# A layer's constants loaded by a generator of their own, one transfer a step, and the gated norm's sums of squares 1.5 later, in a two-layer hybrid decoder trunk

## The chip, the cores and the metric

The kernel runs on one core of one Trainium2 chip. The metric is the device time of one execution in microseconds, taken as the median of the runs; lower is better. Times inside an execution are counted from the start of its span, which runs from its first instruction to its last.

Engines are named as the profile names them: PE (TensorE matmuls; PEld its weight loads), DVE (VectorE), ACT (ScalarE), POOL (GpSimd), SP (SyncE, which here only issues transfers). A name with a q behind it (ACTq, SPq) is the sequencer of that engine: the instructions that it handles itself, the issuing of transfers (DMAs) above all.

## What is computed

Two pre-norm residual layers over 256 tokens of width 1024, all in float32. Each layer normalises the stream, multiplies it with one wide input matrix, runs three causal token mixers beside each other, gates and projects each of them, merges them and adds the result to the stream.

```python
for layer in range(DEPTH):                                   # DEPTH = 2
    h = rms_norm(x, norm_w[layer])
    proj = jnp.einsum('bsd,de->bse', h, w_in[layer])         # 1024 -> 12832 columns
    (a_xbc, a_z, a_dt, b_q, b_k, b_v, b_z,
     c_q, c_k, c_v, c_f, c_z, gates) = jnp.split(proj, split_at, axis=-1)
    y_a = mamba2_branch(a_xbc, a_z, a_dt, conv_w[layer], conv_b[layer], dt_bias[layer],
                        a_log[layer], d_skip[layer], ssm_norm_w[layer])
    y_b = sliding_window_branch(b_q, b_k, b_v, b_z, sinks[layer], cos, sin)
    y_c = forgetting_attention_branch(c_q, c_k, c_v, c_f, c_z, f_bias[layer])
    branch = jnp.einsum('bsiw,iwd->bsid', jnp.stack([y_a, y_b, y_c], axis=2), w_proj[layer])
    g = jax.nn.sigmoid(gates.reshape(b, s, N_BRANCH, d) + gate_bias[layer])
    x = x + jnp.einsum('bsd,de->bse', jnp.sum(g * branch, axis=2), w_out[layer])
return rms_norm(x, final_norm_w)
```

The end of the first mixer is the gated norm that the change touches: four groups of 256 channels, each scaled by the inverse root of its mean square.

```python
y = y + d_skip * xh                                          # d_skip: one number a head
y = y * jax.nn.silu(z)
yf = y.reshape(b, s, 4, 256)
return (yf * lax.rsqrt(jnp.mean(yf * yf, axis=-1, keepdims=True) + NORM_EPS)).reshape(b, s, d) * norm_w
```

## The kernel before

**Tiling.** Weights come in pieces of 512 KB (`raw`, 128 partitions x 1024 numbers), six buffers deep, issued by SP (`load_to`, L336). Each piece is split into a rounded high part `hi` (ACT, L268) and a remainder `lo` (DVE, L269), six buffers each and at most four pieces ahead of PE (`AHEAD`, L32), and three matmul passes (hi x hi, lo x hi, hi x lo; `dense`, L282) give a float32 product. A raw buffer is free for the next transfer once its `lo` is made; a `hi` or `lo` buffer is free once PE has used it for the last time. The program is a list of operations (`ops`): each one computes 128 channels or 128 tokens of one piece into a PSUM buffer (`mm`, three of them), which ACT or DVE then reads. Small products, transposes and scores go to five other PSUM buffers (`mx`).

**Order of the work.** While it is written out, the program keeps a modelled PE time (`clock["t"]`, in microseconds, advanced by `mm` and `transpose`). Everything besides the dense products is a generator, here called a mixer: `launch(br, gen, delay)` (L103) enters it with the time from which it may run, and after each operation `pump` (L130) steps the mixers that are due, the one due longest first. A mixer yields a delay (the constants `D_...`) or a condition. `drain(br)` (L140) runs all mixers of the number `br` to their end at once. PE runs in the order in which this writes its instructions. The other engines are ordered by the scheduler, except for instructions given to `pin` (L262), which keep the order of the program among themselves; the transfers of the constants are pinned, on ACT's sequencer.

**Transfers.** SP issues the weights; ACT's sequencer issues the constants, the gate biases, the residual, and `cumd` and `bias` (the decays of two mixers, written out and read back in another shape). The build gives each of these transfers one of eight completion semaphores in turn, SP's and ACT's together, and a transfer waits on its own sequencer until the last one with the same semaphore has landed. An engine's sequencer goes on in order: while it waits to issue a transfer, the instructions behind it on that engine wait too.

**The constants of a layer** (`layer_consts`, L412 to L430): `vr` (convolution taps and biases, norm weights: 88 rows of 128), `hb` (four vectors of 16 numbers to all 128 partitions), `dsk` (d_skip, twice 64 partitions x 8 numbers; every second number of a row is taken, so each of the 512 numbers of a half is an element of its own in DRAM), and in layer 1 `nwb` (the norm weights, 512 KB, then multiplied by -0.5 on POOL). Layer 0 calls it behind the first key and value products (L1143), layer 1's constants are loaded in the middle of layer 0's third mixer (L1174). `layer_vec` (L432) transposes `vr` on PE and makes small vectors of `hb`; it stands ahead of the second mixer's gates in each layer. `dsk` is first used at L815, `nwb` at L1074.

**The gated norm** (`u_z` with `br == 0`, L838 to L857, and `group_norm`, L850 on): each pair of gates `z` adds the squares of its 256 channels (DVE L842), then launches `group_norm` with the delay `D_GN1`; that sums over the channels with four small products against `ones` on PE, and DVE L855, POOL L858 and DVE L860 to L863 make the scale `gr` of them, which the projection reads at L974 and L976. The line numbers of the kernel after the change are 11 higher from `layer_vec` on.

Of the kernel before, what the change touches and what calls it, by code (L numbers as in the profile page):

```python
# [14 lines left out]
ALU = mybir.AluOpType  # L15

P = 128
S = 256
D = 1024
NK = D // P  # L20
# [3 lines left out]

D_SOFT, D_SOFT2, D_EVAC, D_SSD, D_SSD2 = 7.0, 3.0, 3.0, 8.0, 3.0
D_K, D_Q, D_QK, D_G0, D_FOX, D_BDMA, D_BIAS = 6.0, 5.5, 2.0, 8.0, 0.0, 4.0, 2.0
D_SEL = 2.5
D_GN1, D_CUM, D_H, D_M = 5.0, 12.0, (4.8, 7.0), 5.0
BUDGET = 1.35
T_PP, T_SSD, T_BIAS = 1, 1, 1  # L30
N_RAW, N_SPLIT = 6, 6
# [13 lines left out]
def hybrid_trunk(  # L45
# [5 lines left out]
    nc = tc.nc  # L51
# [11 lines left out]
    def T(tag, shape, dtype=F32, bufs=None):  # L63
        count[0] += 1
        return sb.tile(shape, dtype, tag=tag, name=f"{tag}_{count[0]}",
                       bufs=bufs if bufs is not None else BUFS.get(tag, 1))

    def PS(tag, bufs):
        count[0] += 1
        return ps.tile([P, 512], F32, tag=tag, name=f"{tag}_{count[0]}", bufs=bufs)  # L70
# [4 lines left out]
    def pmx():  # L75
        return PS("mx", 5)
# [22 lines left out]
    def transpose(o, a, i):  # L99
        clock["t"] += 0.109  # L100
        nc.tensor.transpose(o, a, i)  # L101

    def launch(br, gen, delay=0.0):  # L103
        clock["n"] += 1
        waiting.append([clock["t"] + delay, clock["n"], br, gen, None])
# [12 lines left out]
    def allowed(m):  # L118
        return m[4] is None or (tokens[m[4]] > 0 if isinstance(m[4], str) else m[4]())
# [4 lines left out]
    def enter(m):  # L124
        if isinstance(m[4], str):
            tokens[m[4]] -= 1
        m[4] = None
        step(m)
# [11 lines left out]
    def drain(br):  # L140

        left = 0
        while any(m[2] == br for m in waiting):
            for m in sorted(waiting, key=lambda m: (m[0], m[1])):
                if m[2] == br and allowed(m):
                    left += 1
                    enter(m)
                    break
            else:
                m = min((m for m in waiting if allowed(m)), key=lambda m: (m[0], m[1]))  # L150
                left += 1
                enter(m)
        if left and VERBOSE:
            print("drained", br, left, "at", round(clock["t"], 1))
# [107 lines left out]
    def pin(f):  # L262
        return lambda *a, **k: tc.keep_in_program_order(f(*a, **k))  # L263
# [139 lines left out]
    for l in range(L):  # L403
        y = Layer()
# [5 lines left out]
    pdma = pin(nc.scalar.dma_start)  # L410

    def layer_consts(y):  # L412
        l = y.l
        vr = T("vr", [88, P])
        pdma(vr[0:64, :], conv_w[l].rearrange("j (u p) -> (j u) p", p=P))
        pdma(vr[64:80, :], conv_b[l:l + 1, :].rearrange("o (u p) -> (o u) p", p=P))
        pdma(vr[80:88, :], ssm_norm_w[l:l + 1, :].rearrange("o (u p) -> (o u) p", p=P))
        if l:
            y.nwb = T("nwb", [P, D])
            pdma(y.nwb, norm_w[l:l + 1, :].to_broadcast([P, D]))  # L420
            pin(nc.gpsimd.tensor_scalar)(y.nwb, y.nwb, -0.5, None, op0=ALU.mult)
        y.hb = T("hb", [P, 64], bufs=2)
        for i, v in enumerate((dt_bias, f_bias, sinks, a_log)):
            pdma(y.hb[:, 16 * i:16 * i + 16], v[l:l + 1, :].to_broadcast([P, 16]))
        y.dsk = T("dsk", [P, NK], bufs=2)
        for half in range(2):
            src = d_skip[l:l + 1, :].rearrange("o (j two) -> two o j", two=2)[half]
            pdma(y.dsk[64 * half:64 * half + 64, :], src.to_broadcast([64, NK]))
        y.vr = vr

    def layer_vec(y):
        p = pmx()  # L432
        transpose(p[:, 0:88], y.vr, ident[:88, :88])
        y.vec = T("vec", [P, 88], bufs=2)
        act(y.vec[:, 0:80], p[:, 0:80], AF.Copy, scale=0.5)
        act(y.vec[:, 80:88], p[:, 80:88], AF.Copy, scale=-0.5)
        y.nsink = T("nsink", [P, 16], bufs=2)
        pin(ts)(y.nsink, y.hb[:, 32:48], -1.0, None, op0=ALU.mult)
        y.nega = T("nega", [P, 16], bufs=2)
        pin(act)(y.nega, y.hb[:, 48:64], AF.Exp)  # L440
        pin(ts)(y.nega, y.nega, -1.0, None, op0=ALU.mult)
# [167 lines left out]
    def swa_quad(y, c, qT):  # L609
# [64 lines left out]
        tokens["pp"] += 1  # L674
        yield D_SEL
        yield lambda: (1, 2 * c + 1) in y.zdone
# [419 lines left out]
    def sub(src, n=256):  # L1096
        subs.append((src, n))
        return len(subs) - 1
# [5 lines left out]
    for y in layers:  # L1104
        l = y.l
# [32 lines left out]
        if l == 0:  # L1138
            k, v = cols(C_BK), cols(C_BV)
            op(k, u_bkv(y, 0, 0, [lambda j=j: second_rows(j) for j in range(2)]))  # L1140
            op(k, u_bkv(y, 0, 1))
            op(v, u_bkv(y, 256, 0), u_bkv(y, 256, 1))
            op(None, lambda: layer_consts(y0))  # L1143
            for c in (0, 2):
                op(cols(C_BQ + 256 * c, 512), u_bq(y, c, 0), u_bq(y, c, 1))
        else:
            kv, q0 = cols(C_BK, 512), cols(C_BQ)
            op(None, lambda: drain(5))
            op(kv, u_bkv(y, 0, 0))
            op(q0, u_bq(y, 0, 0))  # L1150
            op(None, lambda: drain(6))
            op(kv, u_bkv(y, 0, 1))
            op(q0, u_bq(y, 0, 1))
            for c, n in ((1, 512), (3, 256)):
                op(cols(C_BQ + 256 * c, n), u_bq(y, c, 0), u_bq(y, c, 1))
        op(None, lambda y=y: layer_vec(y))
        op(sub([(0, w[:, C_DT:C_DT + 16]), (16, w[:, C_CF:C_CF + 16])], 32), u_small(y))
        zs(C_ZB, 1)
# [11 lines left out]
        for b, zb in enumerate(((), (0,), (1,), (2, 3))):  # L1170
            op(cols(C_CK + 256 * b), u_ck(y, 2 * b, 0), u_ck(y, 2 * b + 1, P))
            op(cols(C_CQ + 256 * b), u_cq(y, 2 * b, 0), u_cq(y, 2 * b + 1, P))
            if b == 1:
                op(None, load_final if l + 1 == L else lambda: layer_consts(layers[1]))  # L1174
            for z in zb:
                z1(C_ZC, 2, z)
# [4 lines left out]
        o = [sub([(0, w_out[l, :, c:c + n])], n) for c, n in ((0, 256), (256, 512), (768, 256))]  # L1181
# [96 lines left out]
```

## Time and profile before

| what | us |
|---|---|
| median of 3 runs (840.38 to 842.8) | 840.53 |
| the profiled execution, its own device time | 841.65 |
| its span, first to last instruction | 839.8 |
| PE busy in it | 822.7 (98%) |
| DVE busy | 655.9 (78%) |
| ACT busy | 503.3 (60%) |
| POOL busy | 123.4 (15%) |
| DMA, mean | 189 GB/s |

The profile is one execution. Matmuls are pipelined and their ends are modelled, so that a busy PE may still be slowed, by its clock or by short waits between matmuls; a stage is best judged by the time between two points of the program that occur in both layers. "Idle before" in a row is the time that the engine stood before the first instruction of the row, with what ended it.

### The profile page before, as it was taken

Reading aid. Unit: us, or ns where it says so; the run is one execution under the profiler, and the core shown is the slowest. Engines: PE = TensorE matmul, PEld = TensorE weight load, DVE = VectorE, ACT = ScalarE, POOL = GpSimd, SP = SyncE. Lnnn points to the kernel's source line nnn. Section 1 sums busy time; section 2 is a strip of 40 time slices with the busy share of each in tenths; the row PEclk is TensorE's granted clock in tenths of the full one; section 3 lists DMA queues with packets and bytes.
Section 4 is the critical chain, followed back from the end, with each engine's and each line's share of the span. In section 5 each row is a group of like instructions: output and inputs, shape, how many; then the busy total and the mean of one; then the engine's idle time right before and its main releaser. Section 6 shows DMA issues by size and latency. Waiting matters only on the chain.

```text
span 839.8 us, 15652 instructions
## 1 busy us (share of the span) xinstructions
PE 822.7 (98%) x5800; PEld 749.8 (89%) x5800; DVE 655.9 (78%) x1355; ACT 503.3 (60%) x970; POOL 123.4 (15%) x167
## 2 busy tenths in 40 slices
PE   7999999999999999999999999999999999999996
PEld 6989888989989998888989998898899999888896
DVE  5778997998776678876688879979968668788665
ACT  6466777665556675544455668775556667655442
POOL 7411400000211101110014122000003110211000
PEclk9999999999999999999999999999999999999999
DMA  9576565567456546776577455556756564576632
GB/s 304 163 228 201 177 201 164 173 216 226 140 156 212 177 149 189 232 218 215 191 225 242 143 184 171 161 188 211 229 173 181 172 178 150 177 221 216 213 102 74
DMA packets 123595, 158.39 MB, mean 189 GB/s; under 512 B 12784, under 2 KB 84192, under 8 KB 123520
## 3 DMA queue, kind: packets, MB, share of 16 engines
q1 hardware_dynamic: 109456, 140.79, 53.9%
q10 hardware_dynamic: 14016, 16.49, 6.4%
q8 instruction: 45, 0.74, 0.4%
q14 instruction: 30, 0.25, 0.1%
q0 software_dynamic: 48, 0.13, 0.0%
HBM read 155.22 MB, written 2.16 MB: 187 GB/s over the span
## 4 chain that ended last, share of the span: by engine, by line
PE 82%; DVE 7%; DMA 4%; ACT 3%; issue 2%; POOL 1%; ACTq 1%; SPq 0%; POOLq 0%; DVEq 0%
PE mm L97 70%; PE mx L97 9%; DMA raw<-in_w_in_dram 4%; PE mx L101 3%; DVE lo L269 3%; ACT hi L268 1%; POOL sm L858 1%; DVE L L836 1%; DVE L L837 1%; DVE pp L577 1%; DVE pp L559 0%; ACT L L845 0%; ACTq L263 0%; ACT pp L565 0%; DVE L L842 0%
## 5 line engine op out<-in xcount | busy, mean ns | idle before, releaser
L269 DVE TENSOR_TENSOR lo<-raw,hi 128x1024 fp32r<-128x1024 f32 x252 | 310.8, 1247 | 77.4 <-ACT hi L268 71.9
L97 PE MATMUL mm<-hi,L 128*128 128x512 f32 (+1 forms) x1280 | 354.0, 363 | 1.8 <-ACT hi L1209 1.2
L97 PE MATMUL mm<-L,hi 128*128 128x256 f32 x1792 | 318.4, 279 | 0.9 <-DVE L L477 0.9
L268 ACT ACTIVATE hi<-raw 128x1024 fp32r<-128x1024 f32 x252 | 263.3, 1055 | 90.0 <-PE mm L97 68.3
L97 PEld LDWEIGHTS mm<-L,hi 128*128 128x128 f32 x1792 | 278.8, 193 | 6.9 <-issue 3.2
L97 PEld LDWEIGHTS mm<-hi,L 128*128 128x128 f32 x1280 | 229.2, 190 | 30.6 <-issue 2.4
L97 PE MATMUL mm<-L,lo 128*128 128x256 f32 x896 | 247.4, 276 | 0.0
L97 PE MATMUL mm<-lo,L 128*128 128x512 f32 (+1 forms) x640 | 229.4, 359 | 1.4 <-POOL lo L1210 1.4
L97 PEld LDWEIGHTS mm<-L,lo 128*128 128x128 f32 x896 | 172.7, 193 | 0.2
L97 PEld LDWEIGHTS mm<-lo,L 128*128 128x128 f32 x640 | 120.9, 189 | 15.4 <-POOL lo L1210 1.8
L908 POOL TENSOR_SCALAR_AFFINE_SELECT bias<-bias 128x128 f32<-128x128 f32 x64 | 37.3, 614 | 265.4 <-DMA bias<-cumd 265.3
L768 DVE SCALAR_TENSOR_TENSOR L<-L,vec,L 128x255 f32<-128x255 f32 (+2 forms) x96 | 46.9, 489 | 6.1 <-ACT L L765 4.8
L97 PE MATMUL mx<-L,L 128*64 128x128 f32 (+1 forms) x384 | 36.5, 332 | 0.0
L640 ACT ACTIVATE pp<-pp,nm 128x128 f32<-128x128 f32 x64 | 25.2, 394 | 15.6 <-DVE nm L633 12.6
L97 PEld LDWEIGHTS mx<-L,L 128*64 128x64 f32 x384 | 23.8, 137 | 11.9 <-issue 2.7
L565 ACT ACTIVATE pp<-pp,nm 128x128 f32<-128x128 f32 x64 | 28.2, 442 | 7.2 <-DVE nm L559 7.2
L932 ACT ACTIVATE L<-L 128x512 f32<-128x512 f32 x24 | 15.1, 627 | 29.0 <-DVE L L931 28.7
L829 ACT ACTIVATE L<-mm 128x256 f32<-128x256 f32 x48 | 18.0, 375 | 21.1 <-PE mm L97 17.4
L771 ACT ACTIVATE L<-L 128x256 f32<-128x256 f32 x32 | 13.4, 418 | 27.3 <-DVE L L768 26.9
L665 POOL TENSOR_SCALAR_AFFINE_SELECT L<-L 128x256 f32<-128x256 f32 x16 | 10.9, 680 | 107.7 <-ACT L L663 107.7
L633 DVE CUSTOM_DVE_ANT_0 pp<-mx,wmask,nsink 128x128 f32<-128x128 f32 x64 | 24.2, 413 | 1.8 <-PE mx L97 1.8
L858 POOL TENSOR_TENSOR sm<-sm,mhalf 128x4 f32<-128x4 f32 x8 | 10.9, 1363 | 91.8 <-DVE sm L855 91.8
(181 smaller groups left out, 820.8 us busy)
## 6 DMA issues: line engine op xcount, KB each, us to landing
raw<-in_w_in_dram SPq DMA_DIRECT2D x200, 512.0 KB, 4.7
raw<-in_w_proj_dram SPq DMA_DIRECT2D x48, 512.0 KB, 4.6
raw<-in_w_out_dram SPq DMA_DIRECT2D x16, 512.0 KB, 4.8
L<-cumd ACTq DMA_DIRECT2D x8, 512.0 KB, 4.4
bias<-cumd ACTq DMA_DIRECT2D x16, 256.0 KB, 3.7
L<-in_gate_bias_dram ACTq DMA_DIRECT2D x12, 256.0 KB, 3.6
L<-in_x_dram SPq DMA_DIRECT2D x2, 512.0 KB, 6.1
nwb<-in_norm_w_dram SPq DMA_DIRECT2D x1, 512.0 KB, 5.2
```

What stands on the lines that cost most here:

```text
L97: nc.tensor.matmul(o, a, b, **kw)
L101: nc.tensor.transpose(o, a, i)
L268: keep(act)(hi, src, AF.Copy)
L269: keep(tt)(lo, src, hi.bitcast(F32), op=ALU.subtract)
L565: act(pp[:, i, sl], pp[:, i, sl], AF.Exp, scale=-1.0, bias=nm[:, e:e + 1], accum_out=sums[:, e:e + 1])
L633: nc.vector.tensor_tensor_reduce(out=pp[:, i, sl], in0=score(p, i, b), in1=m, scale=-0.125, scalar=ns[:, i:i + 1], op0=ALU.add, op1=ALU.mi ...
L640: act(pp[:, i, sl], pp[:, i, sl], AF.Exp, scale=-1.0, bias=nm[:, e:e + 1], accum_out=sums[:, e:e + 1])
L768: stt(a[:, s:S], x_[:, 0:S - s], y.vec[:, 16 * j + u:16 * j + u + 1], a[:, s:S], op0=ALU.mult, op1=ALU.add)
L829: act(halves(th), p, AF.Tanh, scale=0.5)
L858: nc.gpsimd.tensor_tensor(r0[:, 0:4], v[:, 0:4], mhalf[:, 0:4], op=ALU.pow)
L908: nc.gpsimd.affine_select(out=bias[:, i, dst], in_=bias[:, i, src], compare_op=ALU.is_ge, fill=NEG, base=0, pattern=[[-1, P]], channel_mul ...
L932: act(g, g, AF.Tanh, scale=0.5)
```

## The change

`layer_consts` no longer issues its transfers in one go. It launches a mixer (number 9) that issues one transfer a step with 1.5 of modelled PE time between them (`D_CONST`), in another order: `hb` first, then `vr`, then `dsk`, and in layer 1 `nwb` last, in two halves with 10.0 behind each (`D_NWB`). `layer_vec` runs what is left of it before it uses the constants. `D_GN1` goes from 5.0 to 6.5.

```diff
-D_SEL = 2.5
-D_GN1, D_CUM, D_H, D_M = 5.0, 12.0, (4.8, 7.0), 5.0
+D_SEL, D_CONST, D_NWB = 2.5, 1.5, 10.0
+D_GN1, D_CUM, D_H, D_M = 6.5, 12.0, (4.8, 7.0), 5.0
...
     def layer_consts(y):
+        launch(9, consts(y))
+
+    def consts(y):
         l = y.l
-        vr = T("vr", [88, P])
-        pdma(vr[0:64, :], conv_w[l].rearrange("j (u p) -> (j u) p", p=P))
-        pdma(vr[64:80, :], conv_b[l:l + 1, :].rearrange("o (u p) -> (o u) p", p=P))
-        pdma(vr[80:88, :], ssm_norm_w[l:l + 1, :].rearrange("o (u p) -> (o u) p", p=P))
-        if l:
-            y.nwb = T("nwb", [P, D])
-            pdma(y.nwb, norm_w[l:l + 1, :].to_broadcast([P, D]))
-            pin(nc.gpsimd.tensor_scalar)(y.nwb, y.nwb, -0.5, None, op0=ALU.mult)
+        y.vr = T("vr", [88, P])
         y.hb = T("hb", [P, 64], bufs=2)
+        y.dsk = T("dsk", [P, NK], bufs=2)
         for i, v in enumerate((dt_bias, f_bias, sinks, a_log)):
             pdma(y.hb[:, 16 * i:16 * i + 16], v[l:l + 1, :].to_broadcast([P, 16]))
-        y.dsk = T("dsk", [P, NK], bufs=2)
+            yield D_CONST
+        pdma(y.vr[0:64, :], conv_w[l].rearrange("j (u p) -> (j u) p", p=P))
+        yield D_CONST
+        pdma(y.vr[64:80, :], conv_b[l:l + 1, :].rearrange("o (u p) -> (o u) p", p=P))
+        yield D_CONST
+        pdma(y.vr[80:88, :], ssm_norm_w[l:l + 1, :].rearrange("o (u p) -> (o u) p", p=P))
+        yield D_CONST
         for half in range(2):
             src = d_skip[l:l + 1, :].rearrange("o (j two) -> two o j", two=2)[half]
             pdma(y.dsk[64 * half:64 * half + 64, :], src.to_broadcast([64, NK]))
-        y.vr = vr
+            yield D_CONST
+        if l:
+            y.nwb = T("nwb", [P, D])
+            for j in range(2):
+                hs = slice(j * 512, (j + 1) * 512)
+                pdma(y.nwb[:, hs], norm_w[l:l + 1, hs].to_broadcast([P, 512]))
+                yield D_NWB
+            pin(nc.gpsimd.tensor_scalar)(y.nwb, y.nwb, -0.5, None, op0=ALU.mult)
 
     def layer_vec(y):
+        drain(9)
         p = pmx()
         transpose(p[:, 0:88], y.vr, ident[:88, :88])
```

Below, rows of the built program are shown at three places: an engine's instructions in its order, each with the tile that it writes and those that it reads; [waits DMAHW1_49] is a wait on one of the eight semaphores of transfers, other waits name the engine.

**ACT in layer 0, from the key transpose on** (`L_51` is the key tile, written once for each half of the tokens; `vr`, `hb`, `dsk` the constants; `hi` the split of weights). Before:

```order
L504 ACTIVATE L_51_267<-mx_397 128x4x128 [waits PE_49]
L263 DMA vr_403<-in_conv_w_dram 64x128
L263 DMA vr_403<-in_conv_b_dram 16x128
L263 DMA vr_403<-in_ssm_norm_w_dram 8x128
L263 DMA hb_407<-in_dt_bias_dram 128x16 [waits DMAHW7_49]
L263 DMA hb_407<-in_f_bias_dram 128x16 [waits DMAHW0_49]
L263 DMA hb_407<-in_sinks_dram 128x16 [waits DMAHW1_49]
L263 DMA hb_407<-in_a_log_dram 128x16 [waits DMAHW3_49]
L263 DMA dsk_412<-in_d_skip_dram 64x8x1 [waits DMAHW4_49]
L263 DMA dsk_412<-in_d_skip_dram 64x8x1 [waits DMAHW5_49]
L504 ACTIVATE L_51_267<-mx_428 128x4x128 [waits PE_49]
```

Now (the last transfer of `dsk` follows further down, ahead of `vec`):

```order
L515 ACTIVATE L_51_267<-mx_420 128x4x128 [waits PE_49]
L263 DMA hb_417<-in_f_bias_dram 128x16
L268 ACTIVATE hi_487<-raw_321 128x1024 [waits DMAHW7_49,DVE_49,PE_49]
L268 ACTIVATE hi_499<-raw_327 128x1024 [waits DMAHW0_49,DVE_49,PE_49]
L263 DMA hb_417<-in_a_log_dram 128x16 [waits DMAHW1_49]
L268 ACTIVATE hi_591<-raw_394 128x1024 [waits DVE_49,PE_49]
L268 ACTIVATE hi_603<-raw_466 128x1024 [waits DMAHW2_49,DVE_49,PE_49]
L263 DMA vr_416<-in_ssm_norm_w_dram 8x128 [waits DMAHW3_49]
L537 ACTIVATE qt_438<-mx_533 128x2x128 [waits PE_49]
L537 ACTIVATE qt_446<-mx_537 128x2x128 [waits PE_49]
L263 DMA vr_416<-in_conv_w_dram 64x128 [waits DMAHW6_49]
L263 DMA vr_416<-in_conv_b_dram 16x128 [waits DMAHW7_49]
```

Nine transfers stood in a row between the two halves of the key; now two stand there, and the rest are between splits and copies.

**ACT in layer 0's third mixer, where layer 1's constants are loaded** (`bias` is the decay tile of the next four heads, `qt` a copied key or query, L594 the copy of transposed probabilities, L829 the gate, `nwb` the norm weights). Before:

```order
L263 DMA vr_2962<-in_ssm_norm_w_dram 8x128 [waits DMAHW0_49]
L891 ACTIVATE qt_2860<-mm_2910 128x256 [waits PE_49]
L263 DMA nwb_2966<-in_norm_w_dram 128x1024 [waits DMAHW1_49]
L594 ACTIVATE L_566_2953<-mx_2948 128x512 [waits PE_49]
L263 DMA hb_2969<-in_dt_bias_dram 128x16 [waits DMAHW3_49]
L263 DMA hb_2969<-in_f_bias_dram 128x16 [waits DMAHW4_49]
L263 DMA hb_2969<-in_sinks_dram 128x16 [waits DMAHW5_49]
L263 DMA hb_2969<-in_a_log_dram 128x16 [waits DMAHW6_49]
L263 DMA dsk_2974<-in_d_skip_dram 64x8x1 [waits DMAHW7_49]
L263 DMA dsk_2974<-in_d_skip_dram 64x8x1 [waits DMAHW0_49]
L829 ACTIVATE L_576_3003<-mm_2977 128x256 [waits PE_49]
L594 ACTIVATE L_578_3013<-mx_2955 128x512 [waits PE_49]
```

Now, at the second half of `dsk`, some fifty rows behind the first constant:

```order
L892 ACTIVATE qt_3503<-mm_3466 128x256 [waits PE_49]
L263 DMA dsk_2993<-in_d_skip_dram 64x8x1 [waits DMAHW3_49]
L268 ACTIVATE hi_3575<-raw_3286 128x1024 [waits Activation_49]
L912 DMA bias_3592<-cumd_1044 128x2x256 [waits DMAHW6_49,DMAHW5_49,Pool_49]
L912 DMA bias_3594<-cumd_1044 128x2x256 [waits DMAHW6_49,Pool_49]
L902 ACTIVATE qt_3420<-mm_3516 128x256 [waits PE_49]
L263 DMA nwb_3542<-in_norm_w_dram 128x512 [waits DMAHW0_49]
```

The ten transfers that stood within thirteen rows are now spread over some sixty-five; one half of `dsk` is now directly ahead of two transfers of `bias`, which stood without a constant before them.

**PE in the gated norm, the last group** (`ones` against the summed squares; `mm` is the following gate product, three passes of each 128 rows). Before:

```order
L97 MATMUL mm_787_4217<-lo_776_4188,L8_24_152 128x512
L97 MATMUL mx_789_4245<-ones_8_86,L1_770_4152 128x2 x2
L97 MATMUL mm_794_4257<-hi_752_4066,L8_24_152 128x512
L97 MATMUL mm_794_4257<-hi_752_4066,L8_25_153 128x512
L97 MATMUL mm_794_4257<-lo_753_4067,L8_24_152 128x512
```

Now:

```order
L97 MATMUL mm_789_4246<-lo_756_4086,L8_24_152 128x512
L97 MATMUL mx_796_4271<-ones_8_86,L1_770_4153 128x2 x2
L97 MATMUL mm_789_4246<-hi_772_4170,L8_24_152 128x512
L97 MATMUL mm_789_4246<-hi_772_4170,L8_25_153 128x512
L97 MATMUL mm_789_4246<-lo_773_4171,L8_24_152 128x512
```

The small products of the last group stand in the middle of the gate product that they stood ahead of: twelve matmuls of 512 columns now come before them. Those of the first group, and the six transposes of `pp` behind them, stand 24 matmuls of 256 columns later; the two groups between are where they were. The same holds in layer 1.

## The prediction

> **What bounds the kernel now.** I read the busy times first, then what PE waited for, then stretches that both layers run with the same instructions.
>
> ```profile
> span 839.8 us, 15652 instructions
> PE 822.7 (98%) x5800; PEld 749.8 (89%) x5800; DVE 655.9 (78%) x1355; ACT 503.3 (60%) x970; POOL 123.4 (15%) x167
> ```
>
> PE is busy for 98% of the span and no matmul is removed, so another engine matters only where it makes PE wait. The waits of PE after the start-up (total, times, longest):
>
> ```profile
> PE mx L97 <- DVE L L815: 1.8, 1, 1.8
> PE mx L97 <- DVE L L842: 1.7, 2, 0.9
> ...
> PE mm L97 <- DVE L L477: 0.9, 1, 0.9
> ```
>
> They add up to 4.4 us. What they really cost shows when a stretch is laid beside its twin in the other layer, which has no burst of constants. Columns: window; its length, then busy time (and instructions) of PE, PEld, DVE, ACT, POOL; PE's granted clock; DMA share; GB/s.
>
> ```profile
> 211.26:245.48 34.22, 32.41 (x278) 30.08 (x280) 24.65 (x74) 20.92 (x53) 8.28 (x9) 0.95 0.43 124
> 623.57:653.91 30.34, 30.34 (x278) 28.25 (x280) 23.97 (x70) 19.69 (x48) 7.70 (x8) 1.00 0.61 184
> 47.87:59.21 11.34, 10.46 (x92) 9.45 (x89) 8.95 (x34) 7.47 (x24) 2.30 (x2) 1.00 1.02 324
> 461.59:471.51 9.92, 9.92 (x91) 9.21 (x89) 7.82 (x33) 6.09 (x24) 1.65 (x1) 1.00 0.36 108
> 240.00:245.00 5.00, 4.90 (x28) 4.52 (x29) 5.00 (x26) 3.62 (x16) 0.00 (x0) 0.66 0.04 0
> 289.38:331.35 41.97, 41.10 (x314) 38.00 (x313) 34.83 (x90) 28.63 (x61) 5.47 (x4) 1.00 0.50 153
> ```
>
> The first pair is the third mixer with the same 278 matmuls: layer 0, which loads layer 1's constants there, needs 34.22 - 30.34 = **3.88 us** more, at a mean clock of 0.95. The second pair is the second mixer's first gates: 11.34 - 9.92 = **1.42 us** more in layer 0, behind its own constants. The norm stands alone; its loss is the wait for L842, 1.7 us in two.
>
> **Layer 1's constants.** ACT and its sequencer, with the constants' issues:
>
> ```profile
> 226.11 0.51 ACTq L263 DMA_DIRECT2D vr<-in_conv_w_dram  x1
> ...
> 232.86 1.37 ACTq L263 DMA_DIRECT2D dsk<-in_d_skip_dram  x2
> 234.28 0.38 ACT L829 ACTIVATE L<-mm 128x256 f32<-128x256 f32 x1 [3.49 <-issue]
> ```
>
> From 226.11 to 232.86 + 1.37 = 234.23 the sequencer issues, or waits to issue, ten transfers: 8.1 us. The gate's copy L829 behind them finds ACT idle for 3.49 us; two splits come behind that. DVE takes their remainders ahead of L815, whose buffer PE needs:
>
> ```profile
> 236.61 2.71 DVE L269 TENSOR_TENSOR lo<-raw,hi 128x1024 fp32r<-128x1024 f32 x2 [1.50 <-ACT hi L268]
> ...
> 239.58 0.86 DVE L815 SCALAR_TENSOR_TENSOR L<-L,dsk,mx 128x256 f32<-128x256 f32 x2
> 240.10 0.97 PE L97 MATMUL mx<-qt 64*128 64x128 f32 x6 [1.81 <-DVE L L815]
> ```
>
> PE stands 1.81 us, and the five microseconds from 240 then run at a mean clock of 0.66, 5.00 x 0.34 = 1.70 us of work lost: 3.51 of the 3.88, the rest being scores that start one by one around the gap. Two constants remain in this stretch where ten stood, so layer 0 should run it as layer 1 does: **-3.88**. What covers those two is ACT's slack in the twin, 19.69 us busy of 30.34.
>
> Spreading them brings something new. While `dsk` was under way in layer 0, nothing else moved: here ACT's queue in the 4 us from 36 to 40, what SP's two weight pieces issued in them took to land, and the issue of `bias` in the third mixer while the other `dsk` was under way, and when it was not.
>
> ```profile
> q10 hardware_dynamic: 437, 0.00, 4.8%
> raw<-in_w_in_dram SPq DMA_DIRECT2D x2, 512.0 KB, 14.4
> 245.58 1.93 ACTq L901 DMA_DIRECT2D bias<-cumd  x2
> 269.11 0.37 ACTq L901 DMA_DIRECT2D bias<-cumd  x1
> ```
>
> 437 packets in 4 us are 9.2 ns each; the 512 single numbers of a half are then 4.7 us (an estimate from that row) in which weights stand. One piece is used per 2.7 us (5.36 us a pair of products below), and six are ahead, so that is hidden. But the second half now stands directly ahead of the last two `bias`, and the second of these may hold ACT's sequencer until the half is through, up to 4.7 us. Behind it wait a query's copy, `nwb`, two splits and another copy. PE has three `mm` buffers, 8.0 us of products, `hi` four pieces ahead, and little asked of `mx` there. I take 0; bounds 0 and 4.7 / 8.1 x 3.88 = **+2.2**.
>
> `nwb` in halves is the same bytes; its POOL step moves behind the last `bias` masks, into POOL's idle time ahead of L858:
>
> ```profile
> 236.07 2.79 POOL L263 TENSOR_SCALAR nwb<-nwb 128x1024 f32<-128x1024 f32 x1 [4.24 <-DMA nwb<-in_norm_w_dram]
> 305.34 1.21 POOL L858 TENSOR_TENSOR sm<-sm,mhalf 128x4 f32<-128x4 f32 x1 [29.81 <-DVE sm L855]
> ```
>
> 29.81 us hide 2.79; without them it would be 2.79 on the norm's chain. I take 0.
>
> **Layer 0's own constants.** Two steps of the chain of waits:
>
> ```profile
> 37.16 14.64 DMA raw<-in_w_in_dram
> ...
> 59.45 5.36 PE mm L97 x48
> ```
>
> and two of ACT's splits in that time:
>
> ```profile
> 43.50 1.06 ACT L268 ACTIVATE hi<-raw 128x1024 fp32r<-128x1024 f32 x1 [0.64 <-PE mm L97]
> ...
> 50.40 1.06 ACT L268 ACTIVATE hi<-raw 128x1024 fp32r<-128x1024 f32 x1 [1.25 <-DMA raw<-in_w_in_dram]
> ```
>
> Behind `dsk` the pieces asked for at 36 and 37 took 14.4 us and more. The split of 43.50 still waited for PE alone, that of 50.40 for its piece; the rotations queued behind the remainders on DVE came late with them, and PE waited for those (L477) and for copies behind them on ACT. Now the first half of `dsk` is issued behind the split of 43.50, some 7 us after those pieces; pieces held by it are used 16 us (six times 2.7) later. I take the whole **-1.42**; bounds -1.42 and 0.
>
> The price is `vr`, whose largest transfer is now issued behind two copies of queries:
>
> ```profile
> 39.17 0.66 ACT L526 ACTIVATE qt<-mx 128x256 f32<-128x256 f32 x2 [1.59 <-PE mx L101]
> 47.84 0.24 PE L101 MATMUL mx<-ident,vr 88*128 88x88 f32 x1
> DMA to landing us min/median/max: 2.8/4.7/5.1
> ```
>
> 39.83, two issues of 0.5 and the slowest landing of a `vr`, 5.1, end at 45.9, 1.9 us ahead of PE's transpose at 47.84. I take 0; if it landed as late as weights behind `dsk`, 40.8 + 14.4 = 55.2, PE would stand 7.4 us.
>
> **The gated norm.** PE's small products, the chain behind them, and the same place in layer 1:
>
> ```profile
> 323.03 0.61 PE L97 MATMUL mx<-ones,L 128*128 128x2 f32 x4 [0.87 <-DVE L L842]
> 323.63 6.58 PE mm L97 x30
> 731.42 0.61 PE L97 MATMUL mx<-ones,L 128*128 128x2 f32 x4 [0.82 <-DVE L L842]
> ```
>
> Twelve matmuls now come first, 12 x 6.58 / 30 = 2.6 us, more than either wait: **-1.69**. Late next is the scale `gr`, by 2.6 - 0.9 = 1.7 us; it stays ahead of its readers on DVE, where PE had no wait. The transposes of `pp` that move with the first group leave less room for their copies on ACT:
>
> ```profile
> 304.72 1.07 ACT L594 ACTIVATE L<-mx 128x512 f32<-128x512 f32 x2
> 309.01 1.52 PE L97 MATMUL mx<-L,L 128*64 128x256 f32 x16
> ```
>
> 24 products later is 2.7 us; 304.72 + 1.07 + at most 2.7 = 308.5, and PE wants the copies at 309.01. I take 0; bounds of the part -1.69 and +1.
>
> **The sum.** 3.88 + 1.42 + 1.69 = 6.99. The profiled execution took 841.65, its span of 839.8 and 1.85 around it: 841.65 - 6.99 = 834.7. It lay 1.12 above the median of the runs, so that is 840.53 - 6.99 = **833.5 us** for the median.
>
> **The rivals.**
>
> *The block moves with `dsk`.* ACT stands behind the second half, and 2.2 come back, with PE's half clock 1.70 more: 835.7 to 837.4. For it speaks the 1.93 at 245.58, against it PE's three buffers. Chance 0.15.
>
> *Issuing costs little, the order does the rest.* At about 0.5 each the issues are 5 of the 8.1 us and are still made; if DVE's remainders ahead of L815 are what holds PE, the 3.88 stays: 837.4. Against it, layer 1's twin. Chance 0.07. The Trainium skill ("DMA: Bandwidth & Descriptors", Issuing engines are not separate DMA queues) calls the sequencer's time to initiate a transfer usually small beside the transfer, which would make this rival the rule; ACT's 3.49 us of idling on "issue" disagrees here.
>
> *The half clock stays.* If the clock fell for the thin run of scores and not for the gap, 1.70 remain: 835.2. Against it, the twin runs the same scores at 1.00. Chance 0.04. The Trainium skill ("TensorE: Matmul & The Clock Gate", Why this matters for your kernels) warns of gaps above about 3 us only, so by it 1.81 us would be harmless; the 0.66 right behind the gap disagrees.
>
> *Only the burst goes.* Layer 0's start and the norm find another wait behind the one removed: 840.53 - 3.88 = 836.7. For it, DVE is busy 34.83 of the norm's 41.97 us. Chance 0.08.
>
> *Slower: layer 0 waits for its constants.* `vr` lands behind weights or `dsk`: PE stands 7.4 us at 47.84, 9.1 with the half clock, 833.5 + 9.1 = 842.6. It decides once this wait passes 6.99. Against it, `vr` is issued ahead of `dsk`. Chance 0.06.
>
> **How the numbers follow.** The forecast keeps 0.60. 0.3%, 2.5 us, is about what a measurement of this kernel can tell from no change. All cases but the last lie below 838.0: 0.94, of which I take off 0.05 for mixtures and for the spread of the runs (842.8 among them). Faster 0.89, same 0.07, slower 0.04. The range goes from 1.5 us below the sum to the end of the milder rivals, **832.0 to 837.6**.
>
> **What would show it.** Right: the third mixer's window at 30.3 us and clock 1.00; the first gates at 9.9; no wait of PE for L815, L477 or L842. Wrong: PE waiting for `vr` near 47; a long issue of the last `bias` pair with a PE wait behind it; a PE wait at the moved `ones` or behind the moved `pp`.

## The result, and the profile after

| | before | after |
|---|---|---|
| median, us | 841.66 (840.38 to 843.25, 4 runs) | 834.37 (834.18 to 834.54, 4 runs) |
| ratio after / before | | 0.9912, 95% interval 0.9891 to 0.9934 |
| profiled execution, us | 841.65 | 834.18 |
| its span, us | 839.8 | 832.3 |

The kernel became 0.9% faster, and its runs lie closer together: 0.4 us from the lowest to the highest, where before it was 2.9 (and 5.35 over the 29 runs of before that stand beside experiments further down).

The page of the kernel after, its busy times and its chain of work that ended last:

```profile
span 832.3 us, 15656 instructions
PE 820.6 (99%) x5800; PEld 748.7 (90%) x5800; DVE 656.4 (79%) x1355; ACT 504.6 (61%) x970; POOL 127.2 (15%) x167
...
PE 97%; DMA 1%; ACT 0%; DVE 0%; POOL 0%; SPq 0%; issue 0%; POOLq 0%
```

The same number of matmuls, and the chain is now PE almost throughout. All waits of PE that are left (total, times, longest):

```profile
PE mx L101 <- POOL ident masks.py:199: 1.5, 1, 1.5
PE mm L97 <- ACT hi L1220: 1.4, 1, 1.4
PE mx L101 <- DVE L L1232: 1.3, 1, 1.3
PE mm L97 <- ACT L L268: 0.2, 1, 0.2
PE mm L97 <- DVE L L269: 0.2, 1, 0.2
PE mm L97 <- POOL lo L1221: 0.2, 1, 0.2
```

They belong to the first 13 us; the waits for the gate's product, the rotated key and the squares (L815, L477 and L842 before) are gone. The windows of the two stretches in layer 0 (columns as in the prediction), first from `vr`'s transpose to the first matmul behind the next transposes, then the stretch of layer 0's third mixer that the prediction laid beside its twin, here from the first dense matmul behind the products that began it there to the same point at its end; before and after:

```profile
47.84:59.21 11.37, 10.49 (x92) 9.48 (x90) 8.95 (x34) 7.47 (x24) 2.30 (x2) 1.00 1.02 324
212.64:246.86 34.22, 32.41 (x278) 30.08 (x276) 25.55 (x77) 20.92 (x53) 8.28 (x9) 0.95 0.40 115
```

```profile
47.89:57.84 9.95, 9.95 (x91) 9.29 (x90) 8.09 (x35) 6.02 (x24) 2.30 (x2) 1.00 0.42 130
211.28:241.63 30.35, 30.35 (x279) 28.26 (x277) 24.33 (x72) 20.80 (x53) 7.58 (x8) 1.00 0.60 175
```

In both windows PE is now busy from end to end, at full clock. 11.37 - 9.95 = 1.42 us came from the first (the prediction's 11.34 began one matmul later, at 47.87), 34.22 - 30.35 = 3.87 from the second. From the end of the second to the end of the span it was 839.8 - 246.86 = 592.94 and is 832.3 - 241.63 = 590.67, so 2.27 came from the rest, which holds both gated norms. 1.42 + 3.87 + 2.27 = 7.56; the spans differ by 7.5, since `vr`'s transpose itself now comes 0.05 later (47.89 instead of 47.84). These three numbers, first gates, third mixer and rest, are read for each experiment below.

### The profile page after: what moved, and what is told of

It is laid out like the page before. It is cut to its first block, busy times and chain, and to the rows that moved or that the text cites. A ratio compares the mean times of both kernels' runs of the same rounds, so it can differ in the third digit from the quotient of the medians.

```text
span 832.3 us, 15656 instructions
## 1 busy us (share of the span) xinstructions
PE 820.6 (99%) x5800; PEld 748.7 (90%) x5800; DVE 656.4 (79%) x1355; ACT 504.6 (61%) x970; POOL 127.2 (15%) x167
## 4 chain that ended last, share of the span: by engine, by line
PE 97%; DMA 1%; ACT 0%; DVE 0%; POOL 0%; SPq 0%; issue 0%; POOLq 0%
PE mm L97 83%; PE mx L97 11%; PE mx L101 4%; DMA raw<-in_w_in_dram 1%; POOL lo L1221 0%; ACT hi L1220 0%; ACT L L1079 0%; DVE L L269 0%; ACT L L268 0%; POOLq L1285 0%; ACT L L219 0%; DVE L L1062 0%; SPq L163 0%; DVE L L1067 0%; SPq L164 0%
## 5 line engine op out<-in xcount | busy, mean ns | idle before, releaser
L919 POOL TENSOR_SCALAR_AFFINE_SELECT bias<-bias 128x128 f32<-128x128 f32 x64 | 39.0, 642 | 268.9 <-DMA bias<-cumd 182.4
L651 ACT ACTIVATE pp<-pp,nm 128x128 f32<-128x128 f32 x64 | 25.1, 393 | 13.6 <-DVE nm L644 13.5
```

Source lines behind the costliest of these rows:

```text
L651: act(pp[:, i, sl], pp[:, i, sl], AF.Exp, scale=-1.0, bias=nm[:, e:e + 1], accum_out=sums[:, e:e + 1])
L919: nc.gpsimd.affine_select(out=bias[:, i, dst], in_=bias[:, i, src], compare_op=ALU.is_ge, fill=NEG, base=0, pattern=[[-1, P]], channel_mul ...
```

## The experiments

The profiles of all kernels in one table (us; each is one execution). The line numbers of a kernel depend on the edit; L815, L848 and the like are the gate's product, L842, L853 and L875 the squares.

| kernel | first gates | third mixer | rest | span | median of runs (range) |
|---|---|---|---|---|---|
| before | 11.37 | 34.22 | 592.94 | 839.8 | 841.66 (840.38 to 843.25) |
| after | 9.95 | 30.35 | 590.67 | 832.3 | 834.37 (834.18 to 834.54) |
| norm only | 9.96 | 36.71 | 590.84 | 838.8 | 840.19 (838.58 to 844.43) |
| constants only | 9.96 | 30.35 | 593.04 | 834.7 | 836.55 (836.34 to 837.38) |
| layer 1's constants only | 11.07 | 30.35 | 593.07 | 835.8 | 836.95 (836.43 to 838.24) |
| layer 0's constants only | 9.96 | 34.44 | 593.02 | 838.7 | 840.43 (838.41 to 842.64) |
| no spacing | see there | 30.35 | 590.70 | 837.3 | 838.78 (837.01 to 839.71) |
| before, dense `dsk` | 9.95 | 34.27 | 592.93 | 838.5 | 839.96 (838.07 to 842.66) |
| after, dense `dsk` | 9.96 | 30.35 | 590.77 | 832.4 | 834.29 (834.18 to 836.42) |
| burst on POOL's queue | 10.94 | 30.35 | 593.73 | 836.4 | 838.13 (837.25 to 841.21) |
| layer 1's constants at once | 9.96 | 30.35 | 590.73 | 832.8 | 834.40 (834.14 to 834.69) |
| three other ways | 9.96 | 30.35 | 592.22 | 833.8 | 835.57 (835.45 to 835.88) |

The kernel before had medians of 841.68 (23 runs), 841.83 (29) and 841.97 (11) beside the three groups of experiments (1 to 4, 5 to 8, 9 and 10).

**1. The norm alone**, the kernel before with

```diff
-D_GN1, D_CUM, D_H, D_M = 5.0, 12.0, (4.8, 7.0), 5.0
+D_GN1, D_CUM, D_H, D_M = 6.5, 12.0, (4.8, 7.0), 5.0
```

> The kernel before with D_GN1 at 6.5 alone. Theory: the norm pays for itself and the wait as drawn was too small a price: from the start of the last product's matmul to `ones` 1.25 and 1.20 us went by in the two layers where 0.22 is the pace, and 0.11 more at the restart, so 1.14 + 1.09 = 2.2 us less: span 837.6. Rival: the norm is worth only the two waits of 0.87 and 0.82, and what the whole change gained beyond them came from the constants: span 838.1. A second rival, that it finds the next wait at once: span 839.8, with a wait of PE at the moved `ones`.

The rest of the span took 590.84 where it took 592.94: 2.10 us less, as the theory had it, and not the 1.69 of the two waits. Why is seen in PE's timeline around the last group's small products, before and after:

```profile
321.78 0.38 PE L97 MATMUL mm<-lo,L 128*128 128x512 f32 x1
323.03 0.61 PE L97 MATMUL mx<-ones,L 128*128 128x2 f32 x4 [0.87 <-DVE L L842]
323.50 0.68 PE L97 MATMUL mm<-hi,L 128*128 128x512 f32 x2
```

```profile
319.18 0.38 PE L97 MATMUL mm<-lo,L 128*128 128x512 f32 x1
319.40 0.50 PE L97 MATMUL mx<-ones,L 128*128 128x2 f32 x4
319.76 0.68 PE L97 MATMUL mm<-hi,L 128*128 128x512 f32 x2
```

After, `ones` starts 0.22 behind the start of the matmul ahead of it; before, 1.25. The profile counts the wait only from that matmul's modelled end, 0.38 behind its start, so 0.16 of the 1.03 is missing from it; and the next product starts 0.47 behind `ones` before, 0.36 after. The place costs 1.03 + 0.11 = 1.14, not 0.87.

The span fell by 1.0 only, since the same execution lost more in the third mixer than the profile of before did: 36.71 against 34.22. ACT and PE there, and PE's clock in the microseconds behind the gap:

```profile
234.72 0.38 ACT L829 ACTIVATE L<-mm 128x256 f32<-128x256 f32 x1 [6.08 <-DMA hb<-in_a_log_dram]
```

```profile
240.19 1.65 PE L97 MATMUL mx<-qt 64*128 64x128 f32 x6 [3.29 <-DVE L L815]
```

```profile
244.00:245.00 1.00, 1.00 (x7) 1.00 (x6) 1.00 (x6) 0.39 (x2) 0.00 (x0) 0.50 0.39 121
245.00:246.00 1.00, 1.00 (x8) 1.00 (x8) 1.00 (x2) 0.00 (x0) 0.00 (x0) 0.64 0.80 272
```

The burst held ACT for 6.08 us here instead of 3.49, PE stood for 3.29 instead of 1.81, and half the clock lasted to 245.7. Nothing in the edit touches that place: the size of the burst's price is a matter of the run. This is part of the spread of the runs of before, and it makes the ratio of this experiment (0.9989, 0.9975 to 1.0003) useless for the norm; the stretch decides.

**2. The constants alone**, the kernel after with `D_GN1` back at 5.0.

> The changed kernel with D_GN1 back at 5.0: the constants' mixer alone. Theory (parts add): 3.87 + 1.41 = 5.3 us less than before, span 834.5, PE's two waits for L853 (L842 before) back at 0.8 to 0.9 each and no others. Rival (parts lean on one another): less than 4.5 of it.

Span 834.7, PE's waits for L853 back with 1.7 in two, no other; the ratio was 0.9939 (0.9926 to 0.9952), 5.1 us. The parts add.

**3 and 4. The constants of one layer alone**, both with `D_GN1` at 5.0; `burst` is the function of before:

```diff
     def layer_consts(y):
-        launch(9, consts(y))
+        if y.l == 1:             # experiment 4: y.l == 0
+            launch(9, consts(y))
+        else:
+            burst(y)
```

> Only layer 1's constants (loaded in layer 0's third mixer) come from the mixer, layer 0's in a burst as before; D_GN1 at 5.0. Theory: 3.9 us less, span 835.9, the third mixer's window of layer 0 at 30.4 with the clock at 1.00, the first gates still at 11.3. Rival (layer 0's late start feeds the later gap): less than 3.

> Only layer 0's constants come from the mixer, layer 1's in a burst as before; D_GN1 at 5.0. Theory: 1.4 us less, span 838.4; the first gates at 9.9, and in the third mixer again a gap of PE of about 1.8 for the gate's product with half a clock for some 3 us behind it (34.2). Rival: the gap is an accident of where the weights stand, and 1.4 us earlier it is gone: span near 834.5.

With layer 1's constants alone the third mixer takes 30.35 and the first gates are late (11.07); with layer 0's alone it is the other way round (9.96 and 34.44, a gap of 2.01 and half the clock behind it). The spans lie within 0.3 us of what was expected. The median of experiment 4 cannot be told from that of before (ratio 0.9988, 0.9975 to 1.0001), so there the stretches decide. Its rival fell: the gap does not go away because layer 0 starts earlier. The two stretches have causes of their own.

**5. The mixer without its spacing**, the kernel after with

```diff
-D_SEL, D_CONST, D_NWB = 2.5, 1.5, 10.0
+D_SEL, D_CONST, D_NWB = 2.5, 0.0, 0.0
```

> The changed kernel with D_CONST and D_NWB at 0.0: the mixer and its order of the transfers stay, but all are issued at one point, in a burst. Theory (ACT's sequencer waits in a burst for earlier transfers to land, whatever the order): PE's gap ahead of the scores in layer 0's third mixer comes back with 2 to 3.3 us and half a clock behind it, 34.4 to 36.7 for the stretch that takes 30.3 in the changed kernel, so 4 to 6 us more, 838.4 to 840.7, and the runs spread over more than 3 us again. Rival (the order and the halves of `nwb` do it, not the spacing): 834.4 with a spread of 0.4.

The time was near the theory (838.78) and for another reason, so the theory fell. The third mixer ran in 30.35 although ACT stood idle for 7.43 us there. All was lost in layer 0: `vr`'s transpose came at 52.86 instead of 47.89, 4.97 of the 5.0 us by which the span is longer. ACT, DVE, PE and PE's clock there:

```profile
37.19 3.90 ACT L268 ACTIVATE hi<-raw 128x1024 fp32r<-128x1024 f32 x4 [7.99 <-DMA vr<-in_conv_w_dram]
```

```profile
38.27 3.50 DVE L269 TENSOR_TENSOR lo<-raw,hi 128x1024 fp32r<-128x1024 f32 x3 [5.54 <-ACT hi L268]
41.69 0.42 DVE L485 TENSOR_TENSOR L<-mm,rope 128x256 f32<-128x256 f32 x1
```

```profile
44.27 0.44 PE L101 MATMUL mx<-ident,L 128*128 128x128 f32 x2 [2.29 <-POOL L L528]
45.28 0.44 PE L101 MATMUL mx<-ident,L 128*128 128x128 f32 x2 [0.57 <-POOL L L528]
```

```profile
46.00:47.00 1.00, 1.00 (x5) 0.79 (x4) 0.00 (x0) 0.15 (x1) 0.69 (x1) 0.66 0.43 127
47.00:48.00 1.00, 1.00 (x4) 0.82 (x3) 0.00 (x0) 0.81 (x1) 0.00 (x0) 0.50 0.81 264
...
49.00:50.00 1.00, 1.00 (x4) 0.80 (x3) 0.51 (x1) 0.25 (x1) 0.00 (x0) 0.64 1.10 378
```

Four splits of weights stood behind the burst for 7.99 us. DVE waited 5.54 us for them, and the rotations of the queries (L485 and on) stood behind the remainders on DVE: PE ran out of rotated queries (its waits there are for POOL L528, the rotation's last step), while no wait of PE for a piece of weights or for `vr` is drawn. Of the 4.97 us 2.86 are the two waits, and 1.70 come from half the clock behind them: 0.68 + 2 + 0.72 = 3.40 us at 0.50. So a block of ACT as long as 7 or 8 us is dear at one place and free at another. That gave a new theory, what stands queued behind the burst, and experiment 9.

**6 and 7. `dsk` dense**, in the kernel before and in the one after; what is computed is the same:

```diff
-y.dsk = T("dsk", [P, NK], bufs=2)
+y.dsk = T("dsk", [P, 16], bufs=2)
...
-src = d_skip[l:l + 1, :].rearrange("o (j two) -> two o j", two=2)[half]
-pdma(y.dsk[64 * half:64 * half + 64, :], src.to_broadcast([64, NK]))
+src = d_skip[l:l + 1, half:16]
+pdma(y.dsk[64 * half:64 * half + 64, 0:16 - half], src.to_broadcast([64, 16 - half]))
...
-stt(y.xs[:, u, :], y.xs[:, u, :], y.dsk[:, u:u + 1], py[:, 0:S], ...)
+stt(y.xs[:, u, :], y.xs[:, u, :], y.dsk[:, 2 * u:2 * u + 1], py[:, 0:S], ...)
```

> The kernel before with `dsk` loaded as rows of 15 or 16 neighbouring numbers (column 2u is used) where each half was 512 single numbers: 128 packets instead of 1024. Theory: layer 0's late first gates (1.4 us, in some runs) are `dsk`'s packets alone and go, 9.9 us in every profile; the burst's gap in the third mixer stays, since the sequencer there waits for transfers issued ahead of `dsk`: 0.5 to 1.5 us less than before. Rival: the single numbers are behind both, 5 us less and hardly any spread.

> The changed kernel with the same dense `dsk`. Theory: the single numbers that are left are hidden by the pieces ahead, so no change: 834.4, within 0.3. Rival: something small is still lost to them, 833.5 or less.

In the kernel before the dense `dsk` was worth 1.9 us, a little more than the theory's 1.5 (ratio 0.9977, 0.9962 to 0.9993): the first gates took 9.95, the third mixer 34.27 as before. The table alone would not do, since the first gates were on time in experiment 1 as well, with the single numbers. The view of the transfers from 30 to 50 us shows the cause. Each digit is the busy share of the DMA engines in half a microsecond, before and with the dense `dsk`:

```profile
DMA  9986986421000000000000000000038999999999
...
raw<-in_w_in_dram SPq DMA_DIRECT2D x6, 512.0 KB, 14.3
```

```profile
DMA  9978764111157998999999999996200002759998
...
raw<-in_w_in_dram SPq DMA_DIRECT2D x8, 512.0 KB, 6.3
```

From 35 to 44 the weights stand with the single numbers, and a piece lands in 14.3 us; with the dense form they flow and take 6.3. ACT's splits in that time wait for PE alone again (43.57, 44.86, 46.16, 47.45), where before two of those that followed that of 43.50 waited for their pieces (50.40 and 51.91). In experiment 1 the same dead time was broken up at 39 us, one split still waited 3.05 us for its piece, and PE was just not reached: the margin is that thin. After the change nothing is left to gain there (834.29, as expected); the dead time is still in its trace, 44 to 50 us, and the pieces ahead cover it.

**8. The burst on another sequencer**, the kernel before with

```diff
-    pdma = pin(nc.scalar.dma_start)
+    pdma = pin(nc.gpsimd.dma_start)
```

> The kernel before with the constants' ten transfers of each layer still in a burst, but issued from POOL's queue. Theory (what costs is that ACT's sequencer stands): the third mixer of layer 0 runs in 30.4 us, 3.9 to 6 us less; the start of layer 0 stays as it was, so 835.5 to 837.5 in all. Rival (the transfers themselves get in the way of the weights, wherever they are issued): the third mixer stays at 34 or more and the time at 841.

```profile
212.32:242.67 30.35, 30.35 (x278) 28.26 (x276) 24.34 (x73) 20.72 (x53) 7.84 (x8) 1.00 0.61 176
47.95:58.89 10.94, 10.06 (x91) 9.35 (x90) 10.13 (x35) 7.47 (x24) 2.31 (x2) 1.00 1.05 338
```

```profile
95.61 0.56 POOL L263 DMA_DIRECT2D vr<-in_conv_w_dram  x1
...
107.70 1.41 POOL L263 DMA_DIRECT2D dsk<-in_d_skip_dram  x2
```

The ratio was 0.9965 (0.9950 to 0.9980), the median 838.13, 0.6 above the theory's range. The third mixer has its 30.35, but this does not decide between the theory and the rival: the scheduler, which is bound only to the order of these transfers among themselves, put layer 1's burst at 95.6 to 109.1 us, more than 100 us ahead of the third mixer, and the trace shows no transfer of POOL's queue from 200 to 250 us. The stretch lost its burst, the issues and the traffic alike. What tells the two apart is the burst on ACT as four traces have it, ordered by how long ACT stood ahead of the gate's copy (L829; L862 in experiment 4):

| kernel | ACT idle | PE's gap | third mixer |
|---|---|---|---|
| before | 3.49 | 1.81 | 34.22 |
| before, dense `dsk` (6) | 4.10 | 1.85 | 34.27 |
| layer 0's constants only (4) | 4.54 | 2.01 | 34.44 |
| norm only (1) | 6.08 | 3.29 | 36.71 |

The longer ACT stands, the longer PE's gap. With the dense `dsk` the weights issued from 222 to 250 us landed in 4.3 us, where before they took 11.1, and the gap is no shorter: the single numbers are not behind it. The chain that the prediction shows (the gate's copy, two splits, their remainders, L815, PE) also waits for no weights. So ACT's sequencer it is; a run with all ten transfers at that place and off ACT was not made.

Layer 0's burst did stay at its place (25.7 to 31.9 us), and with `dsk` in single numbers the first gates were late although ACT did not stand: there ACT is not the cause.

The Trainium skill ("DMA: Bandwidth & Descriptors", Issuing engines are not separate DMA queues) holds that issuing on several engines saves only the sequencer's time, usually small beside the transfer; in the third mixer that time, 8.1 us of ACT's sequencer in the profile of before, is what the 3.87 hung on.

**9. Layer 1's constants at once**, the kernel after with every `yield` in `consts` 0.0 in layer 1.

> The changed kernel, but layer 1's eleven transfers are issued in one go where their mixer starts; layer 0's stay spaced. Theory, formed after the run without spacing (what counts is what stands queued on ACT behind the burst: there ACT idled 7.43 us and PE lost nothing, and all that was lost was lost at the start of layer 0): 834.4 again, the third mixer at 30.35, spread under 1 us. Rival (that run's third mixer was luck, a burst of this size costs by itself): 836 to 840 in some runs, spread over 2 us.

```profile
241.03 0.39 ACT L840 ACTIVATE L<-mm 128x256 f32<-128x256 f32 x1 [7.95 <-PE mm L97]
```

```profile
211.72:242.07 30.35, 30.35 (x279) 28.26 (x277) 20.30 (x60) 15.70 (x37) 7.81 (x8) 1.00 0.50 142
```

ACT idles for 7.95 us in the middle of the third mixer and PE loses nothing, in the profile and in six runs (834.14 to 834.69). The mixer begins its transfers 19.2 us into the stretch (230.90 - 211.72), right behind a gate's copy, and two copies of probabilities pass after its second issue, before the long waits. The burst of before began at 13.5 (226.11 - 212.64), and the same gate's copy and the same two copies stood behind the whole of it (234.28 and 234.56). For layer 1's constants the place does it; the spacing is not needed. (The order of the transfers differs too and was not tried by itself, but ACT stands longer here than before, and nothing that PE needs soon stands behind it.)

**10. The same three causes, taken away in other ways**: the kernel before with the burst on POOL's queue (8), the dense `dsk` (6) and `D_GN1` 6.5 (1), no mixer for the constants.

> The kernel before, no mixer for the constants, with each suspected cause taken away in another way: the burst is issued from POOL's queue (so that ACT's sequencer never stands), `dsk` is loaded dense (so that its single numbers hold no weights), D_GN1 is 6.5. Theory (these three are all of it): first gates 9.95, third mixer 30.35, from there to the end 590.7: span 832.3 and 834.4, as the changed kernel. Rival (the changed kernel's order of the transfers gives something of its own, or POOL's queue takes something): 836 or more.

Layer 1's burst is again issued far ahead of the third mixer (95.0 to 108 us). All three stretches of PE are as in the kernel after, and so is the last transfer's issue, but the span is 1.5 longer. Of the kernel after, and of this one:

```profile
828.97 0.34 ACTq L1080 DMA_DIRECT2D out_dram<-L  x1
```

```profile
span 833.8 us, 15667 instructions
...
828.94 0.34 ACTq L1069 DMA_DIRECT2D out_dram<-L  x1
```

From that issue to the end it takes 4.9 us instead of 3.3 (in experiment 8, 836.4 - 832.45 = 3.95; before, 3.4). The nineteen transfers that now go over POOL's queue come with a longer end of the program; why was not tried. So taking away the burst on ACT, the single numbers and the early `ones` is all of the gain in front of it, and with POOL's queue 1.2 us of it are given back (835.57 against 834.37).

## Why the prediction was right, and where it was off

The direction, the three places and the range (832.0 to 837.6) held. Step by step:

- **Layer 1's constants**, -3.88 foreseen, 3.87 measured, at clock 1.00 as layer 1's twin. ACT's sequencer as the cause rests on the four traces beside experiment 8, the clock's part on the windows. That the two numbers agree to 0.01 says only that the stretch now runs as its twin does (30.35 and 30.34): both loss figures come from the same profile of before. The step "spreading them" was less exact than its number: experiment 9 shows that the later start of the mixer is enough. The price itself is no constant, 3.87 in the profile of before, 3.92, 4.09 and 6.36 in experiments 6, 4 and 1.
- **Layer 0's constants**, -1.42 foreseen, 1.42 measured, and `dsk`'s single numbers as the cause are shown by experiment 6. Here the spacing does matter: at once, at the mixer's place and in its order, they cost 4.97 (experiment 5). `vr` came in time, transposed at 47.89 with no wait. This loss, too, is not in every execution: experiment 1, with layer 0's burst unchanged, ran its first gates in 9.96.
- **The gated norm** is the term that was mis-sized: 1.69 foreseen, 2.27 measured. The step took the two waits as the profile draws them; each place cost 0.27 more, of the matmul's modelled end and of the restart. The bounds (-1.69 and +1) did not hold it.
- **The base of the sum** was the other step that failed, and the larger one. The 6.99 came out of an execution of 841.65 and was taken off a median of 840.53, as if the 1.12 between them had nothing to do with the change. It had: the losses differ from run to run, and once they are gone the runs end close together (834.18 to 834.54). And 840.53 was the median of three runs only; with more it is 841.66 to 841.97. 841.65 - 7.5 = 834.15 is what came; 840.53 - 6.99 = 833.54 is 0.83 too low: 1.12 from the base, less 0.48 by which the profiled execution fell further than foreseen (834.18 instead of 834.66, the norm above all), and the median after lies 0.19 above its profiled execution. Base and norm erred in opposite directions; that they partly cancelled was luck.
- **The rivals.** "The block moves with `dsk`": ACT's two issues of `bias` behind the second half took 1.05 and held nobody. "Issuing costs little": the issues are still made on ACT, and the third mixer takes 30.35. "The half clock stays": 1.00 in the window; and in experiment 5 half a clock followed a gap with no scores near it. "Only the burst goes": all three went. "Layer 0 waits for its constants": no wait at 47.89. Experiment 5 shows that layer 0 can lose 4.97 to its constants in one go, but to what stands queued behind them on ACT and DVE, not to `vr`.
- The rule of the Trainium skill on gaps above about 3 us ("TensorE: Matmul & The Clock Gate", Why this matters for your kernels) does not go far enough here: gaps of 1.81 (before), 1.85, 2.01 and 2.29 us (experiments 6, 4 and 5) were each followed by half the clock.

## What to carry to other kernels

A block of an engine's sequencer is priced first by what stands queued behind it, and only then by its length: eight idle microseconds of ACT cost nothing behind the copies that PE needs next, while 3.5 to 6.1 ahead of them cost 3.9 to 6.4. An issue that is moved to another engine's sequencer may also move in time: look where it landed before reading the result. Where a loss varies from run to run, subtract it from the execution that shows it, and expect the spread to go with it. A wait of PE as the profile draws it can be too small (0.87 of 1.14 here); the distance between the starts of the two matmuls, less the usual one, is the loss.

## What was not expected of the hardware

- **Half the clock after short gaps, for a fixed time.** PE's clock in the microseconds after the gap of 1.81 (before), of 2.01 (experiment 4), and around that of 3.29 (experiment 1, 236.90 to 240.19; its end is shown there):

```profile
240.00:241.00 1.00, 0.90 (x6) 0.52 (x6) 1.00 (x7) 0.32 (x2) 0.00 (x0) 0.92 0.05 0
241.00:242.00 1.00, 1.00 (x5) 1.00 (x5) 1.00 (x7) 1.00 (x7) 0.00 (x0) 0.50 0.05 0
...
244.00:245.00 1.00, 1.00 (x10) 1.00 (x10) 1.00 (x6) 0.30 (x2) 0.00 (x0) 0.87 0.03 0
```

```profile
239.00:240.00 1.00, 1.00 (x6) 0.61 (x6) 1.00 (x8) 0.52 (x3) 0.00 (x0) 0.59 0.06 0
...
242.00:243.00 1.00, 1.00 (x8) 1.00 (x8) 1.00 (x3) 1.00 (x6) 0.00 (x0) 0.71 0.03 0
```

```profile
238.00:239.00 1.00, 0.00 (x0) 0.00 (x0) 1.00 (x2) 1.00 (x2) 0.00 (x0) 0.94 0.05 0
239.00:240.00 1.00, 0.00 (x0) 0.00 (x0) 1.00 (x3) 1.00 (x2) 0.00 (x0) 0.50 0.05 0
```

  Counted as time at 0.50, the first is 0.16 + 3 + 0.26 = 3.42 us, the second 0.82 + 2 + 0.58 = 3.40. In experiment 1 it is 0.12 + 6 + 0.72 = 6.84, twice as long, 5.5 of it behind the restart of PE at 240.19. It begins 0.75 us behind the restart in the first, 0.3 in the second, and 1.3 ahead of it, inside the gap, in experiment 1, so it is not tied to the restart. All five spells (those of experiments 5 and 6 are 3.40 and 3.42) are one or two times 3.4 us, as if the clock were set for that long at a time; what decides it was not tried. Gaps up to 1.11 (the squares of layer 1 in experiment 8) left the clock at 1.00. Where between 1.11 and 1.81 it begins was not tried.
- **1024 single numbers, 4 KB in all, can stop 512 KB pieces for some 9 us** (35 to 44 us in the view of experiment 6), from another engine's queue.
- **The issue of a small transfer waits for an earlier one's landing**: ten issues, most of 0.3 to 0.7 us, took 8.1 in the profile of before, and ACT's idle times of 6.08 (experiment 1) and 7.99 (experiment 5) ended with such a landing. This makes the price of the burst vary, 3.87 to 6.36 in four profiles; how much of the runs' spread of 5 us it is was not shown.
